# One more seven-product group, the SSM inputs one block earlier, and the samples' attention columns in a lane of their own

## The chip, the cores and the metric

The kernel runs on one core of a Trainium2 chip. The metric is the device time of one execution in microseconds (us); the profiled execution and the timed ones are executions of the same program.

## The reference

One layer of a hybrid decoder trunk, for a prompt of 16 meta tokens and 512 new tokens and for 8 samples of one new token each (536 token columns in all, of which 520 are needed in the output). Everything is float32.

```python
xn = rmsnorm(x, norm_gain)
q, k, v, z_a, u, z_s, g_a, g_s = split(xn @ w_in)        # 2048 -> 8704
q, k = rope(rmsnorm(q)), rope(rmsnorm(k))                  # 16 query heads, 4 key heads, 64 wide
o_attn = sink_attention(q, k, v)          # prompt: window 128 and 16 meta keys; samples: their caches
y_ssm  = s5_branch(u)                     # 64 groups of 16, 64 complex states, scan over time, gelu
y_ssm  = y_ssm * sigmoid(y_ssm @ w_glu + b_glu)
br_a = (o_attn * silu(z_a)) @ w_attn_out
br_s = (y_ssm * silu(z_s)) @ w_ssm_out
y = x + (sigmoid(g_a) * br_a + sigmoid(g_s) * br_s) @ w_out
```

The new keys, values, caches and SSM states are outputs as well.

## The kernel before

**How a product is made.** Weights come from memory in units of 1024 x 128 (a "unit": 8 tiles of 128 x 128). ScalarE rounds a unit to `whi` (line 1019 or 1085), VectorE makes the remainder `wlo` (line 1020 or 1086); the activations are split in the same way. TensorE adds three products, high by high, high by low and low by high, so one block of 128 output columns over 2048 inputs is 96 matmuls of 260 or 268 columns (`mm`, line 1179), and over 1024 inputs 48. Units are made two ahead in three buffers (class `Stream`).

**Groups.** A pair of output blocks over 2048 inputs can be made as a group of seven products instead of eight (class `Quads`, function `quad`, Winograd's form of Strassen's scheme): 7 x 24 = 168 matmuls (line 1415) where two plain blocks have 192. VectorE adds weights for it (line 1084) and makes seven `wlo` instead of four. `NQ` is the number of groups in the input projection; the last product, by w_out, is eight groups.

**The order of the program.** It is written as one main line of matmul blocks:

1. five blocks while x arrives, then `NA` = 4 plain blocks;
2. `NQ` = 16 groups (groups 9 to 12 are the query heads, the others gates);
3. sixteen plain blocks in the order of the string in `ORDER1`: `u` an input block of the SSM branch, `h` a block of keys or values, `x` a gate block;
4. the gate blocks that are left (`while nx < 47`), and the last one by hand;
5. "GLU": 8 blocks over the SSM's output, 48 matmuls each, whose results (`Y2`, made by line 1756, a ScalarE cast and line 1699 on VectorE) are the input of 6; the first unit of 6 needs the eighth of them for its last six matmuls;
6. "sD": 16 blocks by w_ssm_out, 48 matmuls each;
7. "A": 16 blocks by w_attn_out, 48 matmuls each, whose input is the attention's output `oT`, split into `A` (lines 1698 and 1699);
8. eight groups by w_out.

**Background.** The SSM blocks, the attention and the samples' attention are Python generators in three lanes (class `Background`). After every few matmuls the main line calls `bg.step(budget)`; each `yield c` costs c of the credit, and `yield None` ends a lane's turn for this step. The budget is a number per 8 matmul steps (6.4 up to the attention, then `BUDGET2` = 6.0 in 4, `BUDGET3` = 3.4 in 5, `BUDGET4` = 4.8 in 6). It counts matmuls of the main line, not time. Ahead of 7, `bg.drain()` runs whatever is left with no matmul of the main line to go beside it. While `bg.fair` holds, lanes take turns; `attention()` sets it to False, and then the first lane goes ahead of the others.

**The background's parts.** `ssm_consts` and `ssm_block` run for eight blocks; block n is put in line when its `u` block is made. `attention()` begins when they are done and the head norms are made: `values`, `keys`, then for each of 4 key heads `queries` and four blocks. A block (kv, b) is `scores` (lines 816 and 817 on TensorE, in two halves that share one bank of PSUM: ScalarE copies a half at line 820, VectorE masks it at line 822), `softmax` (VectorE lines 828 and 829, ScalarE's four exponentials at 832, VectorE 834 and 839, ScalarE's four scalings at 838), `turn` (TensorE's transposes at 847 and 848, VectorE 851, ScalarE 853 and 857) and `weigh` (TensorE 865, VectorE 870). Scores of a block are issued ahead of `turn` and `weigh` of the block before it. `NDELAY` is a number of steps that the first block waits.

**Samples.** `sample_heads` and `sample_weigh` (16 passes over the key cache, 16 over the value cache, VectorE lines 659 and 660) run in lane 2; the lane is added in `attention()`. At the end of `attention()`, after the last block, `at.sample` loads the result and the gates of the samples (tile `zs`, which shares a buffer with `dV` of the blocks), transposes (line 930) and writes the samples' 8 columns of `oT` (line 935).

Engines run their instructions in the order in which the program issues them; that order is fixed when the program is built.

Of the kernel before, what the change touches and what calls it, by code (L numbers as in the profile page):

```python
# [8 lines left out]
F32 = mybir.dt.float32  # L9
# [5 lines left out]
P = 128  # L15
# [321 lines left out]
def ssm_consts(nc, pool, dram, R, D, ub, a_bT, a_bN, a_cT, e32, d_skip, later, free):  # L337

    v = nc.vector
# [13 lines left out]
    bN, c = R["next"]  # L353
# [55 lines left out]
    yield 1.4  # L409
    yield None  # L410

    kp = R["kp"]
    yield None
    with later():
        for a in range(4):
            for i in range(2):
# [270 lines left out]
class Attn:  # L687
# [225 lines left out]
            with self.later():  # L913
                self.weigh(*self.held, *parts)

    def sample(self, oD):

        nc, pool, v = self.nc, self.pool, self.nc.vector
        o = pool.tile([P, 2, 64], F32, name="o_s", tag="sv")
        for n in range(2):  # L920
            nc.gpsimd.dma_start(out=o[:, n], in_=oD)
        zs = pool.tile([P, 8, 2, 4], F32, name="zs", tag="dV", bufs=1)
        for c in range(2):
            nc.gpsimd.dma_start(out=zs[:, :, c], in_=self.gates[:, :, 260 * c + 256:260 * c + 260].rearrange("b p w -> p b w"))
        yield None
        yield None
        yield None
        ps = self.psum.tile([P, 2, 512], F32, name="aux")
        with self.later():
            nc.tensor.transpose(out=ps[:, 0, 0:128], in_=o.rearrange("p a d -> p (a d)"), identity=self.C["idn"])  # L930
        for e in range(2):
            part = slice(64 * e, 64 * e + 64)
            src = ps[part, 0, 0:128].rearrange("p (c j b e) -> p e b c j", c=2, j=4, e=2)[:, e]
            for c in range(2):
                v.scalar_tensor_tensor(out=self.oT[part, :, c, 256:260], in0=src[:, :, c], scalar=4.0, in1=zs[part, :, c],
                                       op0=ALU.mult, op1=ALU.mult)
        yield 0.0
# [7 lines left out]
BUDGET2, BUDGET3, BUDGET4 = 6.0, 3.4, 4.8  # L945
HIGH = 4000
NLOAD = 3
NDELAY = 4
ATTC = (("kg", 1), ("kgs", 1), ("qg", 1), ("qgs", 1), ("mown", P), ("mprev", P), ("bd64", 4), ("sink", 16))
NXR = 10  # L950
NWARM = 9

NA, NQ = 4, 16
QHEADS = range(9, 13)
XORDER = (list(range(16, 25)) + list(range(16)) + list(range(32, 8 + 2 * NQ)) + list(range(25, 32))
          + list(range(8 + 2 * NQ, 48)))
ORDER1 = [(k, 0) for k in "xuhuhuhuhuxuxuxu"]
for _k in "hu":
    for _n, _i in enumerate([i for i, o in enumerate(ORDER1) if o[0] == _k]):
        ORDER1[_i] = (_k, _n)  # L960
# [139 lines left out]
def trunk(tc, A, O):  # L1100
    nc = tc.nc
# [239 lines left out]
    def heads(i, sb=None):  # L1341
# [22 lines left out]
        def sums():  # L1364
            if i > 3:
                ps = aux.tile([P, 2, 512], F32, name="aux")[:, 0]
            else:
                if "ax" not in S:
                    S["ax"] = aux.tile([P, 2, 512], F32, name="aux")
# [16 lines left out]
    def head_norms():  # L1386
# [7 lines left out]
        def finish():  # L1394
            for r1, dst, p, n in rows:
                r2 = ev.tile([p, n], F32, name="z")
                v.tensor_scalar(out=r1, in0=r1, scalar1=1.0 / 64, scalar2=1e-6, op0=ALU.mult, op1=ALU.add)
                rsqrt_dve(nc, ev, r2, r1, [p, n], "z", "")
                nc.sync.dma_start(out=flat2(dst, n), in_=r2)
            normed.append(1)  # L1400

        return finish

# [2 lines left out]
    def samples():  # L1406
        qk = yield from sample_heads(nc, smpl, dram, smc, C["idn"], rawD, rkD, rqD, S["ax"][:, 1, P:],
                                     lambda: tc.issue_after(bg.last))
        smp.extend(qk)
        smp.extend((yield from sample_weigh(nc, smpl, dram, *qk, A["ssk"], A["kc"], A["vc"], lambda: tc.issue_after(bg.last))))  # L1410

    def product(bank, W, x, first, ps=range(8)):
        for p in ps:
# [177 lines left out]
    for n_, (kind, n) in enumerate(ORDER1):  # L1591
# [9 lines left out]
        if sp is None:  # L1601
# [12 lines left out]
            S["ax"] = S.get("ax") or aux.tile([P, 2, 512], F32, name="aux")  # L1614
            S["bu"] = [aux.tile([P, 512], F32, name=n) for n in ("tr", "wg")] + [S["ax"][:, 0]]
            S["kp"] = S["ax"][:, 1, 0:P]
# [4 lines left out]
        uf = sp.tile([P, 2, CH], F32, name="uf", bufs=1)  # L1621
        with tc.high_priority(offset=HIGH):
            v.tensor_tensor(out=uf, in0=ps, in1=R_, op=ALU.mult)
        uD = dram.tile([P, 2 * CH], F32, name="uD", bufs=8)
        nc.gpsimd.dma_start(out=uD, in_=flat(uf))
        uDs[n] = uD
# [2 lines left out]
    def attention():  # L1629
# [2 lines left out]
            yield None  # L1632
        bg.fair, bg.cap = False, 2.0
        bud[0] = BUDGET2
        bg.add(samples(), lane=2)
        nc.sync.dma_start(out=O["pst"], in_=S["pst"])
        nc.sync.dma_start(out=O["sst"], in_=S["sst"])
        spool.__exit__(None, None, None)
# [29 lines left out]
        for kv in range(4):  # L1668
# [7 lines left out]
                for _ in range(NDELAY):  # L1676
                    yield None
            yield from at.blocks(kv, kv == 3)
        while len(smp) < 3:
            yield None  # L1680
        yield from at.sample(smp[2])
        yield from attended()


# [310 lines left out]
```

## Time and profile before

| | us |
|---|---|
| median of 3 runs (1259.73 to 1260.58) | 1259.96 |
| the profiled execution | 1259.92 |
| its span, first to last instruction | 1258.1 |
| TensorE busy in the span | 1245.8 (99%) |
| VectorE | 986.4 (78%) |
| ScalarE | 632.5 (50%) |
| GpSimd | 324.4 (26%) |

PE is TensorE, DVE VectorE, ACT ScalarE, POOL GpSimd, SP the queue that issues most DMAs. A row of the chain gives start, length, engine, output tile, line and number of instructions; a row of waits gives the waiting instruction, what it waited for, and total us, times and longest us; a row of windows gives, after the stretch, its length and then busy us and number of instructions of PE, PE's weight loads, DVE, ACT and POOL, the granted clock, the DMA share and GB/s; a row of the timeline gives start, length, engine, line, operation, output and input tiles and, in brackets, the idle time before it and what ended it.

### The profile page before, as it was taken

How to read it: one execution, taken by the hardware profiler on the slowest of the kernel's cores; microseconds unless marked ns; L12 is line 12 of the kernel's file. 1: busy time of each engine (PE TensorE's matmuls, PEld its weight loads, DVE VectorE, ACT ScalarE, POOL GpSimd, SP SyncE). 2: the span in 40 equal slices, each digit the busy share in tenths (PEclk: the TensorE clock that was granted, in tenths of full speed). 3: DMA queues.
4: the chain of work that ended last, by engine and by line, in shares of the span. 5: the costliest groups of instructions: out<-in, count | busy, mean ns of one | idle time of the engine just before them, and what ended most of it. 6: DMA issues, size and time to landing. Idle time of an engine off the chain costs nothing.

```text
span 1258.1 us, 26470 instructions
## 1 busy us (share of the span) xinstructions
PE 1245.8 (99%) x10333; PEld 1221.6 (97%) x10333; DVE 986.4 (78%) x1516; ACT 632.5 (50%) x1351; POOL 324.4 (26%) x541
## 2 busy tenths in 40 slices
PE   9999999999999999999999999999999999999998
PEld 9999999999999999999999999999999899999998
DVE  8687878888898756778689858899987477887875
ACT  8554444444445587555552233657665433344342
POOL 0003999940000015337345132112111000000000
PEclk9999999999999999999999999999999999999999
DMA  8544443444464475557556479777667466555441
GB/s 294 198 162 149 138 144 110 143 127 162 153 195 154 144 241 175 176 167 180 170 145 173 124 232 278 244 218 230 215 201 240 151 195 190 166 186 168 143 138 51
DMA packets 99872, 222.42 MB, mean 177 GB/s; under 512 B 17324, under 2 KB 36868, under 8 KB 99716
## 3 DMA queue, kind: packets, MB, share of 16 engines
q1 hardware_dynamic: 86500, 191.97, 47.3%
q0 software_dynamic: 13248, 28.77, 8.9%
q8 instruction: 81, 1.33, 0.4%
q14 instruction: 43, 0.35, 0.1%
HBM read 183.17 MB, written 38.43 MB: 176 GB/s over the span
## 4 chain that ended last, share of the span: by engine, by line
PE 89%; issue 4%; DMA 3%; DVE 2%; POOL 1%; ACT 1%; SPq 0%; DVEq 0%; ACTq 0%; POOLq 0%
PE mm L1179 41%; PE pr L1415 37%; PE mm L1271 2%; PE wg L865 1%; PE aux L1415 1%; PE aux L1179 1%; DMA cache<-in_kc 1%; PE aux L1271 1%; DMA KH<-KH 1%; PE wg L537 1%; PE tr L537 1%; PE aux L816 1%; DMA qD<-x 1%; PE tr L478 0%; PE aux L817 0%
## 5 line engine op out<-in xcount | busy, mean ns | idle before, releaser
L1085 ACT CAST whi<-raw 128x1024 fp32r<-128x1024 f32 x168 | 173.2, 1049 | 167.8 <-DVE raw L1084 68.9
L1086 DVE TENSOR_TENSOR wlo<-raw,whi 128x1024 fp32r<-128x1024 f32 x168 | 206.7, 1251 | 56.4 <-ACT whi L1085 56.0
L1019 ACT CAST whi<-raw 128x1024 fp32r<-128x1024 f32 (+3 forms) x124 | 118.4, 964 | 147.1 <-PE mm L1179 70.7
L1415 PE MATMUL pr<-tau,whi 128*128 128x260 f32 x992 | 180.1, 283 | 0.0
L1179 PE MATMUL mm<-xh,whi 128*128 128x260 f32 (+1 forms) x744 | 172.8, 286 | 0.2 <-ACT xr L1244 0.2
L1179 PE MATMUL mm<-xh,wlo 128*128 128x260 f32 (+1 forms) x744 | 172.2, 285 | 0.0
L1179 PE MATMUL mm<-xl,whi 128*128 128x260 f32 (+1 forms) x744 | 171.8, 285 | 0.0
L1020 DVE TENSOR_TENSOR wlo<-raw,whi 128x1024 fp32r<-128x1024 f32 (+3 forms) x124 | 137.6, 1118 | 32.6 <-ACT whi L1019 32.1
L1415 PE MATMUL pr<-cb,whi 128*128 128x260 f32 x848 | 153.0, 283 | 0.0
L1415 PEld LDWEIGHTS pr<-tau,whi 128*128 128x128 f32 x992 | 152.7, 188 | 0.0
L1415 PE MATMUL pr<-tau,wlo 128*128 128x260 f32 x496 | 139.4, 282 | 0.0
L1415 PEld LDWEIGHTS pr<-cb,whi 128*128 128x128 f32 x848 | 130.8, 188 | 0.2 <-ACT z L1449 0.2
L1179 PEld LDWEIGHTS mm<-xh,whi 128*128 128x128 f32 x744 | 123.6, 188 | 1.6 <-issue 1.2
L1179 PEld LDWEIGHTS mm<-xl,whi 128*128 128x128 f32 x744 | 123.8, 188 | 0.4 <-issue 0.4
L1179 PEld LDWEIGHTS mm<-xh,wlo 128*128 128x128 f32 x744 | 123.4, 188 | 0.2 <-issue 0.2
L1084 DVE TENSOR_TENSOR raw<-raw 128x1024 f32<-128x1024 f32 x95 | 118.7, 1250 | 1.4
L1415 PE MATMUL pr<-cb,wlo 128*128 128x260 f32 x424 | 119.1, 283 | 0.2 <-DVE wlo L1086 0.2
L1415 PE MATMUL pr<-xl,whi 128*128 128x260 f32 x376 | 105.1, 282 | 0.0
L1415 PE MATMUL pr<-xh,wlo 128*128 128x260 f32 x376 | 105.0, 283 | 0.0
L1179 PE MATMUL mm<-Y,whi 128*128 128x260 f32 x576 | 104.4, 287 | 0.3 <-ACT t L1755 0.3
L1415 PE MATMUL pr<-xh,whi 128*128 128x260 f32 x376 | 104.3, 284 | 0.0
L1415 PEld LDWEIGHTS pr<-tau,wlo 128*128 128x128 f32 x496 | 93.1, 188 | 0.0
(432 smaller groups left out, 3022.9 us busy)
## 6 DMA issues: line engine op xcount, KB each, us to landing
raw<-in_w SPq DMA_DIRECT2D x202, 512.0 KB, 4.4
gD<-z SPq DMA_DIRECT2D x36, 260.0 KB, 3.1
t<-gD SPq DMA_DIRECT2D x32, 260.0 KB, 3.4
cache<-in_vc POOLq DMA_DIRECT2D x16, 286.0 KB, 3.4
cache<-in_kc POOLq DMA_DIRECT2D x15, 288.0 KB, 4.8
xr<-in_x SPq DMA_DIRECT2D x16, 268.0 KB, 6.0
xg<-in_x SPq DMA_DIRECT2D x8, 536.0 KB
sbw<-rawD SPq DMA_DIRECT2D x16, 260.0 KB, 6.8
```

The lines of the kernel that those rows point to most:

```text
L537: nc.tensor.matmul(o[n], lhsT=D["CL"][:, 2 * e + n, i, 1:5], rhs=H[:, 2 * e + n, i, 0:140], start=False, stop=(i == 1))
L816: nc.tensor.matmul(ps[:, e, 0:272], lhsT=q, rhs=KH[:, k0:k0 + 272], start=True, stop=False)
L865: nc.tensor.matmul(pv[64 * e:64 * e + 64, 0:256], lhsT=V, rhs=pr[:, e::2], start=(i == 0), stop=(i == len(parts) - 1))
L1019: nc.scalar.copy(out=hi, in_=raw)
L1020: self.dve = nc.vector.tensor_tensor(out=lo, in0=raw, in1=hi.bitcast(F32), op=ALU.subtract).ins
L1084: nc.vector.tensor_tensor(out=o, in0=o, in1=i, op=ALU.add)
L1085: nc.scalar.copy(out=hi, in_=t)
L1086: self.dve = nc.vector.tensor_tensor(out=lo, in0=t, in1=hi.bitcast(F32), op=ALU.subtract).ins
L1179: m = nc.tensor.matmul(ps[:, c, 0:W], lhsT=wt[:, k], rhs=xo(kt, c), start=f, stop=l)
L1271: nc.tensor.matmul(ps[:, c, 0:260], lhsT=wt[:, kt % 8], rhs=xk(xo, kt, c, 8), start=f, stop=l)
L1415: m = nc.tensor.matmul(bank, lhsT=wt[:, p], rhs=x(p, e), start=first and f and p == 0, stop=l and p == 7, skip_group_check=not first and l ...
```

## The change

It moves four things. `NQ` goes from 16 to 17, so two gate blocks that stood in step 4 become a group of step 2; `XORDER` and the layout of the weights follow. The string in `ORDER1` puts each `u` one block earlier (first block of step 3 instead of second), and the PSUM tiles that the SSM shares (`S["ax"]`, `S["bu"]`, `S["kp"]`) are made after the first `u` block. `samples()` is put in lane 2 as soon as the head norms are made, makes its heads while lanes take turns, waits there for `bg.fair` to end, and makes the samples' columns of `oT` itself, in its own pool, as soon as the gates of key head 3 are made; `attention()` waits for that at its end. `NDELAY` goes from 4 to 6.

```diff
@@ ssm_consts
+    yield None
+    while "kp" not in R:
+        yield None
     kp = R["kp"]
-    yield None
@@ Attn.sample
-    def sample(self, oD):
-        nc, pool, v = self.nc, self.pool, self.nc.vector
-        o = pool.tile([P, 2, 64], F32, name="o_s", tag="sv")
+    def sample(self, pool, oD):
+        nc, v = self.nc, self.nc.vector
+        o = pool.tile([P, 576], F32, name="ozs", tag="cache")
+        zs = o[:, 128:192].rearrange("p (b c j) -> p b c j", b=8, c=2)
+        o = o[:, 0:128].rearrange("p (n d) -> p n d", n=2)
         for n in range(2):
             nc.gpsimd.dma_start(out=o[:, n], in_=oD)
-        zs = pool.tile([P, 8, 2, 4], F32, name="zs", tag="dV", bufs=1)
...
-NDELAY = 4
+NDELAY = 6
-NA, NQ = 4, 16
+NA, NQ = 4, 17
-ORDER1 = [(k, 0) for k in "xuhuhuhuhuxuxuxu"]
+ORDER1 = [(k, 0) for k in "uxuhuhuhuhuxuxux"]
@@ head_norms, finish
             normed.append(1)
+            bg.add(samples(), lane=2)
@@ samples
         smp.extend(qk)
+        while bg.fair:
+            yield None
         smp.extend((yield from sample_weigh(...)))
+        while not at.gated(3):
+            yield None
+        yield from at.sample(smpl, smp[2])
+        smp.append(True)
@@ trunk, ORDER1's loop: made after the first u block's uf, not ahead of its matmuls
+        if n == 0:
+            S["ax"] = aux.tile([P, 2, 512], F32, name="aux")
+            S["bu"] = [aux.tile([P, 512], F32, name=nm) for nm in ("tr", "wg")] + [S["ax"][:, 0]]
+            S["kp"] = S["ax"][:, 1, 0:P]
@@ attention
-        bg.add(samples(), lane=2)
...
-        while len(smp) < 3:
+        while len(smp) < 5:
             yield None
-        yield from at.sample(smp[2])
         yield from attended()
```

New line numbers are up to seven higher than old ones: 816, 847, 865 and 1179 of before are 818, 849, 867 and 1182 now, and on VectorE 659, 660, 800, 1699, 1756 and 1768 are 661, 662, 802, 1706, 1763 and 1775.

Where things stand in TensorE's order, counted in matmul instructions of the program from its start (a float32 one counts once):

| | before | now |
|---|---|---|
| the last group of step 2 ends | 3619 | 3781 |
| first product of the SSM's constants (`kp`) | 3830 | 3959 |
| last product of the SSM's eighth block | 5799 | 6061 |
| first scores of the attention | 6160 | 6477 |
| the second GLU block begins | 6518 | 6446 |
| the first sD block begins | 6914 | 6815 |
| last matmul of sD | 7871 | 7773 |
| last `weigh` of the attention | 7835 | 7847 |
| all | 8854 | 8830 |

The first place is TensorE's order at the end of sD, where A begins. `mm<-Y` is sD, `mm<-A` is A; `aux<-KH` and `aux<-KL` are scores, `tr` and `wg<-k_idn` transposes, `wg<-po`, `wg<-pm` and `wg<-pp` a block's `weigh`. Before:

```order
L1179 MATMUL mm<-Y_10688,wlo 128x260 x2
L865 MATMUL wg<-po,dV 64x256 x2
L865 MATMUL wg<-pm,Vm 64x256 x2
L865 MATMUL wg<-pp,V 64x256 x2
L1179 MATMUL mm<-Y_10688,whi 128x260 x4
L1179 MATMUL mm<-Y_10688,wlo 128x260 x2
...
L1179 MATMUL mm<-Y2q,whi 128x260 x2
L1179 MATMUL mm<-Y_10688,wlo 128x260 x2
L1179 MATMUL mm<-A_12788,whi 128x260 x6
```

Now:

```order
L867 MATMUL wg<-pp,V 64x256 x2
L849 MATMUL tr<-k_idn,Pn 128x128 x4
L1182 MATMUL mm<-Y_10636,wlo 128x260
L818 MATMUL aux<-KH_9340,QT_11876 128x272
L819 MATMUL aux<-KL_9344,QT_11876 128x272
...
L849 MATMUL tr<-k_idn,Pn 128x128
L933 MATMUL aux<-k_idn,ozs 128x128
...
L867 MATMUL wg<-po,dV 64x256 x2
L867 MATMUL wg<-pm,Vm 64x256 x2
L867 MATMUL wg<-pp,V 64x256 x2
L1182 MATMUL mm<-A_12692,whi 128x260 x6
```

Before, the last block's `weigh` stood 36 matmuls of sD ahead of A. Now the single sD matmul shown is the last, and 74 matmuls of the attention stand between it and A: scores of the blocks (3, 1), (3, 2) and (3, 3), four sets of transposes, five sets of `weigh`, and the samples' transpose.

The second place is VectorE's order from the last block of GLU (`z<-t,z`, the product with the gate) to its `Y2q`, which sD's first unit needs. Before:

```order
L1756 SCALAR_TENSOR_TENSOR z<-t,z 128x520
L800 TENSOR_TENSOR QT_11102<-sbw,QT_11102 64x512
L829 TENSOR_SCALAR m<-m 128x4
L822 COPY_PREDICATED S<-k_attc,aux 128x2x128
L800 TENSOR_TENSOR QT_11105<-sbw,QT_11105 64x512
L1699 TENSOR_TENSOR Y2q<-z,Y_10688 128x520
```

Now:

```order
L1763 SCALAR_TENSOR_TENSOR z<-t,z 128x520
L662 TENSOR_REDUCE o_s<-cache 128x4
L725 SCALAR_TENSOR_TENSOR sbw<-sbw,k_attc 128x520
L841 TENSOR_TENSOR Pm<-S,den 128x64
L802 TENSOR_TENSOR QT_10399<-sbw,QT_10399 64x512
L726 SCALAR_TENSOR_TENSOR sbw<-sbw,k_attc 128x520
L872 TENSOR_TENSOR oT<-wg,zr 128x2x2x32 x2
L824 COPY_PREDICATED S<-k_attc,aux 128x2x128
L802 TENSOR_TENSOR QT_10432<-sbw,QT_10432 64x512
L1706 TENSOR_TENSOR Y2q<-z,Y_10636 128x520
```

Four rows stood between the two; now there are eight (nine instructions), a pass over the value cache and a query's rope among them. From the first such product of GLU to the eighth VectorE has 89 instructions before and 89 now, but not the same ones: line 659 has four more of the value cache and three fewer of the key cache, line 660 three more of the one and two fewer of the other, lines 723, 724 and 726 one more each, 732 two more, 800 two more; 828, 839 and 903 have one fewer each, 851 two fewer, 870 four fewer (line numbers of before). On TensorE 60 matmuls of the background stand among GLU's second to eighth block before, and 33 now.

More of the change, by code (lines that the diff above doesn't have):

```diff
@@ L1367, in sums @@
             else:
-                if "ax" not in S:
-                    S["ax"] = aux.tile([P, 2, 512], F32, name="aux")
                 ps = S["ax"][:, 1, P:]
@@ L1613, in trunk @@
                 nc.gpsimd.memset(t, 0.0)
-            S["ax"] = S.get("ax") or aux.tile([P, 2, 512], F32, name="aux")
-            S["bu"] = [aux.tile([P, 512], F32, name=n) for n in ("tr", "wg")] + [S["ax"][:, 0]]
-            S["kp"] = S["ax"][:, 1, 0:P]
             bg.add(ssm_states(nc, sc, sp, S, A["h0"]), lane=1)
```

## The prediction

> **What bounds the kernel now.** I read the page's busy times first, then the chain for TensorE's pace, TensorE's waits, windows over the stages, and last the timeline of one attention block. The page:
>
> ```profile
> span 1258.1 us, 26470 instructions
> PE 1245.8 (99%) x10333; PEld 1221.6 (97%) x10333; DVE 986.4 (78%) x1516; ACT 632.5 (50%) x1351; POOL 324.4 (26%) x541
> ```
>
> TensorE is never free for long, so the time is the number of matmuls times their pace, plus the places where TensorE waits. Rows of the chain give the pace and the end of the attention:
>
> ```profile
> 57.80 55.62 PE mm L1179 x464
> 139.04 158.99 PE pr L1415 x1323
> 443.92 7.99 PE aux L1179 x67
> 469.73 0.59 PE aux L417 x16
> 889.40 1.01 PE wg L865 x8
> 982.39 1.45 PE wg L865 x12
> 992.05 0.91 POOL zs L924
> ...
> 998.82 0.63 ACT A L1698
> 999.55 92.65 PE mm L1179 x768
> ```
>
> Both 55.62 / 464 and 158.99 / 1323 are 0.120 us a matmul: a plain block of 96 is 11.5 us, a group of 168 is 20.2 us. The last three rows show why A starts at 999.55: the load of the samples' gates `zs` goes out last, at 992.05, then come the split and TensorE. TensorE's waits between 735 and 1000 us, and three stretches (groups; GLU from the first to the eighth product `z`; around A's start):
>
> ```profile
> PE mm L1179 <- ACT A L1698: 2.4, 1, 2.4
> PE aux L816 <- DVE QT L800: 2.0, 1, 2.0
> PE aux L816 <- DVE S L822: 0.7, 2, 0.5
> ...
> ```
>
> ```profile
> 113.40:437.70 324.30, 324.30 (x2702) 321.51 (x2701) 275.18 (x309) 155.06 (x219) 146.62 (x202) 1.00 0.45 146
> 828.50:878.40 49.90, 49.47 (x404) 46.65 (x403) 46.99 (x91) 32.60 (x88) 10.08 (x14) 1.00 0.73 223
> 950.00:1000.00 50.00, 47.57 (x389) 43.92 (x387) 26.13 (x52) 23.25 (x69) 4.88 (x8) 1.00 0.59 191
> ```
>
> VectorE is busy 46.99 of 49.9 us in GLU (94%), where TensorE still does not wait. So there are two places with little to spare: VectorE in GLU, and whatever is left of the attention when sD ends, since nothing of the main line covers it. Both meet the change.
>
> **The change part by part.** The sum goes against the profiled execution, 1259.9 us; the median of the runs is 1259.96, so no correction.
>
> *The seventeenth group.* Two plain blocks of 192 matmuls become 168: 24 x 0.120 = -2.9 us. Its three extra casts, three extra `wlo` and four weight sums lie beside 20.2 us of matmuls, on a VectorE that is busy 275 of 324 us in that stage and a ScalarE busy half of it: nothing. If that cover failed, a group would be late by the wait for one `wlo`, about 1 us.
>
> *What the group takes away.* Those two blocks stood where the attention runs. The budget is counted in matmuls, so the background gets 2 x 2 x 6.0 = 24 us of credit less behind the groups. The `u` blocks one earlier should give half of it back, but the order shows they don't: the SSM's last product stands 2280 matmuls behind the end of the groups now and 2180 before, the first scores 1370 ahead of A's start instead of 1711, and 74 matmuls of the attention are left when sD is over. That is the drain. TensorE there has to wait for ScalarE and VectorE, whose work on one block is, in the timeline (ScalarE, then VectorE, then TensorE):
>
> ```profile
> 971.97 0.40 ACT L820 COPY S<-aux 128x288 f32<-128x288 f32 x1 [1.97 <-PE aux L817]
> 974.43 0.42 ACT L832 ACTIVATE S<-S,m 128x145 f32<-128x145 f32 x1 [2.06 <-DVE m L829]
> ...
> 975.95 0.19 ACT L832 ACTIVATION_READ_ACCUMULATOR S<-S,m 128x1 f32 x1
> 976.05 0.56 ACT L857 COPY pp<-tr 128x512 f32<-128x512 f32 x1
> 976.51 1.04 ACT L1019 CAST whi<-raw 128x1024 fp32r<-128x1024 f32 x1
> 977.46 0.99 ACT L838 ACTIVATE Pn<-S,den 128x128 f32<-128x128 f32 x3
> 978.35 1.11 ACT L853 ACTIVATE pm<-wg,k_attc 64x128 f32<-64x128 f32 x4
> ```
>
> ```profile
> 972.40 0.45 DVE L822 COPY_PREDICATED S<-k_attc,aux 128x256 f32<-128x256 int32 x1 [1.61 <-ACT S L820]
> 972.96 0.76 DVE L828 TENSOR_REDUCE m<-S 128x4 f32<-128x580 f32 x1
> 973.75 0.49 DVE L870 TENSOR_TENSOR oT<-wg,zr 128x128 f32<-128x128 f32 x2
> 974.15 0.16 DVE L829 TENSOR_SCALAR m<-m 128x4 f32<-128x4 f32 x1
> 974.33 0.69 DVE L851 TENSOR_TENSOR po<-tr,k_attc 128x512 f32<-128x512 f32 x1
> 976.49 0.17 DVE L834 RECIPROCAL den<-den 128x4 f32<-128x4 f32 x1
> 976.95 0.22 DVE L839 TENSOR_TENSOR Pm<-S,den 128x64 f32<-128x64 f32 x1 [0.29 <-PE wg L848]
> ```
>
> ```profile
> 957.66 0.28 PE L816 MATMUL aux<-KH,QT 128*128 128x272 f32 x1
> ...
> 958.15 0.28 PE L1179 MATMUL mm<-Y2q,whi 128*128 128x260 f32 x1
> 973.63 0.66 PE L847 MATMUL tr<-k_idn,Pn 128*128 128x128 f32 x4
> ```
>
> ScalarE's queue from the end of sD on: six copies of scores (2.4), four times four exponentials (974.43 to 976.14, 1.7 each: 6.8), four sets of scalings (1.3 each: 5.1), five `pm` (5.6), four `pp` (2.3), one weight cast (1.0) and the first split (0.6): 23.8 us without a gap, the lower end. One block alone, nothing overlapped, is two halves of scores at 1.65 (TensorE 0.5, 0.40, 0.45 and hand-overs), 0.9 to the maximum and its scaling, 1.7, 0.4 on VectorE, 1.3, transposes 0.7, 1.8 for `pm` and `po`, 1.45 of `weigh`, 0.5: 12 us; three of these and 2 us for block (2, 3) are 38, the upper end. Going through the rows in their order, each starting when its engine and its input are there, I come to 29 us from sD's last matmul to A's first; it lies nearer the lower end because scores of the next block stand ahead of a block's `turn`. Of these 29 us TensorE's own rows are 12 (six halves at 0.49; `weigh` four times 1.45 and once 1.01; transposes and `Pm` about 2.5), which it did before as well, under cover. So the drain costs 17 us net, between 12 and 26.
>
> *Waits that go.* A's 2.4 us (the old end of the attention) are replaced by the drain: -2.4. The 2.0 us for the first `QT` goes, since two more steps of delay put 48 matmuls, 5.8 us, ahead of those scores: -2.0, or 0. The 0.7 us at scores and what is smaller I leave as they are.
>
> *GLU.* Its eight blocks now carry other background. TensorE from the first to the eighth product `z`: 336 matmuls are 40.4 us, and 33 background ones (24 of scores at 0.123, a `weigh`, transposes) 4.5: 45 us, where 60 stood before and it took 49.2. VectorE's 89 instructions there add up to 2.1 us more than before (four cache multiplies of 0.75 for three of 0.76, reductions, rope at 0.75, `QT` at 0.69, less `po`, `oT`, a maximum): 49 to 51 us. It falls behind by 4 to 6 us. Before, it ran behind by about 4 throughout (`z` after its tanh; the last row, of a table by line, is the cache multiply's mean):
>
> ```profile
> 823.41 0.69 ACT L1755 ACTIVATE t<-mm,k_bglu 128x520 f32<-128x520 f32 x1
> 828.51 0.69 DVE L1756 SCALAR_TENSOR_TENSOR z<-t,z 128x520 f32<-128x520 f32 x1
> ...
> 873.39 0.71 ACT L1755 ACTIVATE t<-mm,k_bglu 128x520 f32<-128x520 f32 x1
> 877.71 0.70 DVE L1756 SCALAR_TENSOR_TENSOR z<-t,z 128x520 f32<-128x520 f32 x1
> 880.43 0.70 DVE L1699 TENSOR_TENSOR Y2q<-z,Y 128x520 fp32r<-128x520 f32 x1
> ...
> L659 DVE TENSOR_TENSOR cache<-cache,ssc 128x572 f32<-128x572 f32 x16 | 11.6, 749 | 0.0
> ```
>
> The last `Y2q` came 2.0 us behind its `z`; the rows between them now add up to 4.9. So it is ready 0.7 + 0.7 + 5.3 us plus the lag behind GLU's end, and sD's first unit needs it after 42 matmuls and 9 of the background, 6 us. With a lag of 4 to 10 TensorE waits 4.5 to 10.5 us, once, at sD's beginning; I take 7, with 3 to 10 as ends.
>
> *`u` first.* The constants' first product came 25.8 us behind the end of the groups (469.73 - 443.92), behind 210 matmuls or 25.2 us; now 178 or 21.4 stand ahead of it. If the loads and casts for it take as long as before TensorE waits up to 4.4 us; nothing if they follow the order. I take 1, since much of that chain begins with the groups' end in both.
>
> *Samples' lane.* Their columns no longer stand behind the last block. On GpSimd's queue the result's load goes out after the two copies of the windows, as before, six blocks ahead of its use: hidden. If it were late, TensorE's transposes behind the samples' one would wait with it in the drain. No instruction is added; the wait in lane 2 is one of the builder, not of an engine.
>
> Sum: 1259.9 - 2.9 - 2.4 - 2.0 + 17 + 7 + 1 = 1277.6. I say 1277 us.
>
> A rule of the Trainium skill bears on both waits. In the trace the granted clock is 1.00 in every window, also in the one with the 2.4 us wait. The skill (TensorE: Matmul & The Clock Gate, "What's actually happening") says that an idle window of about 3.4 us halves TensorE's clock until a busy window has passed. By it a single wait of 7 us, and perhaps the drain, would each be followed by some 3.4 us at half rate, an estimated 1.7 us each, so 1279 to 1281; no run here has a wait that long.
>
> **The rivals.** *The drain is as cheap as blocks were before* (the other side). The sixteen blocks before made TensorE wait 0.7 us for masked scores, and if the handing over in the drain cost no more, its 12 us of rows would take 13: 1277.6 - 16 = 1261.6. It decides below a net drain of 1.9 us, where the time comes within 0.2% of before. For it: the rows are the same ones. Against it: from 889.40 to 982.39 eight blocks took 11.6 us each then, filled with sD; ScalarE alone needs 23.8. 5 in 100.
>
> *VectorE catches up in GLU.* It was idle 6% of that stretch; if the lag at GLU's first block is nil and rows overlap better, sD's first unit finds `Y2q` ready: 1270.6, with the drain's ends 1266 to 1279. 20 in 100.
>
> *The drain is serial*: in-order queues line the blocks up, 38 us, net 26: 1286.6. For it: both halves of scores share one bank, and ScalarE's copy of the next half often stands behind `pm` or the exponentials. 12 in 100.
>
> *The clock falls.* If TensorE ran at half its pace for as long as the wait at sD's beginning lasted, 7 us hold 29 matmuls instead of 58: +3.5, and as much behind the drain: up to 1284.6. Against it: 1.00 everywhere so far. 10 in 100.
>
> **How the numbers follow.** The forecast with both waits (1271 to 1284) has 53 in 100. Cases that end above 1262.5 are slower by more than 0.2% (2.5 us, about what this kernel's measurement tells from no change): all but the first rival's 5 in 100, of which 4 lie in the band and 1 below it (a drain that cheap with a lag absorbed too), and one more below it for what I have not seen: slower 0.94, same 0.04, faster 0.02. The range 1266 to 1288 leaves out the first rival and the tails of the second and third.
>
> **What would show it.** Groups: 168 matmuls more at line 1423 (and 192 fewer at 1182), same pace. The chain at the end of sD through ScalarE and VectorE, with TensorE's waits on scores, `Pn` and `pm` and 25 to 33 us from sD's last matmul to A's first. A wait of TensorE on VectorE's `Y2q` (line 1706) at sD's beginning. No wait on `zs`. Wrong would be: A within 20 us of sD's end, or no wait at sD's beginning and a low lag of `z`.

## The result, and the profile after

The changed kernel takes 1274.32 us (median of four runs, 1272.49 to 1276.49) where the kernel before took 1260.06 beside it: ratio 1.0113, 95% interval 1.0095 to 1.0132. The profiled execution took 1275.33 us, a span of 1273.6, 15.5 more than before. The page's first lines:

```profile
span 1273.6 us, 26432 instructions
PE 1248.9 (98%) x10309; PEld 1222.0 (96%) x10309; DVE 995.2 (78%) x1526; ACT 635.8 (50%) x1358; POOL 320.3 (25%) x541
```

TensorE has 24 matmuls fewer than before, as the group should have it (1056 rows of `pr<-tau,whi` for 992), and yet it is busy 3.1 us longer. Its idle time, span less busy, went from 12.3 to 24.7 us. So the 15.5 us are 12.4 of new waits, less 2.9 for 24 matmuls at 0.120, which leaves 6.0 for rows that ran slower. Stage by stage, first before, then after: from the groups' end to GLU's first matmul; GLU and sD; from sD's last matmul to A's first (columns as before: length, busy us and number for PE, PE's weight loads, DVE, ACT, POOL, then granted clock, DMA share, GB/s):

```profile
443.90:811.70 367.80, 365.05 (x3075) 359.58 (x3073) 281.39 (x543) 192.95 (x569) 146.02 (x281) 1.00 0.66 193
811.70:997.10 185.40, 184.74 (x1497) 170.46 (x1495) 149.14 (x287) 114.15 (x326) 27.81 (x45) 1.00 0.67 211
997.10:999.50 2.40, 0.01 (x1) 0.00 (x0) 1.20 (x5) 0.68 (x2) 0.00 (x0) 1.00 0.12 6
```

```profile
464.10:805.10 341.00, 335.83 (x2846) 332.10 (x2844) 260.15 (x505) 173.36 (x521) 150.33 (x287) 1.00 0.67 189
805.10:986.80 181.70, 178.38 (x1437) 167.53 (x1438) 150.06 (x281) 107.49 (x293) 21.51 (x40) 0.99 0.73 232
986.80:1014.90 28.10, 18.06 (x103) 10.49 (x101) 14.44 (x43) 20.66 (x78) 0.38 (x2) 0.88 0.20 66
```

The groups end 20.2 us later (one group more); the first stage shown is 26.8 us shorter, the second 3.7, and the time from A's first matmul to the end is the same (258.6 and 258.7). The third is the drain: 28.1 us for 2.4, with 18.06 us of TensorE in it and a granted clock of 0.88. Of the 12.4 us of idle time 7.6 lie in the drain, 2.4 ahead of GLU and 2.7 in GLU and sD. TensorE's waits, over the whole span:

```profile
PE mm L1182 <- ACT Y L1705: 4.6, 1, 4.6
PE wg L850 <- DVE Pm L841: 2.3, 2, 1.2
PE aux L818 <- DVE S L824: 2.0, 2, 1.1
PE aux L818 <- DVE QT L802: 1.8, 1, 1.8
...
PE tr L480 <- DMA kD<-k: 0.6, 1, 0.6
```

The largest is new and was not forecast: GLU's first block waits 4.6 us for `Y1`, the SSM's output. Its loads go out when the last gate block has done with `xl`, and the rest of that block covers them: 9.9 us before (801.8 to 811.7, with rows of the attention in it), 6.9 now (793.6 to 800.45, with none of them). They also land later. The same four of the eight loads, with the casts that ScalarE makes of them, before and then after (least, median and greatest ns of one, then the first and the last start in us):

```profile
L1731 SPq DMA_DIRECT2D Y<-yD x4: 382/470/937, 802.3 to 804.2; - x4
L1698 ACT CAST Y<-Y x4: 625/628/632, 807.4 to 811.1; 128x520 fp32r<-128x520 f32 x4
```

```profile
L1738 SPq DMA_DIRECT2D Y<-yD x4: 320/490/693, 794.0 to 796.7; - x4
L1705 ACT CAST Y<-Y x4: 617/622/625, 804.4 to 808.3; 128x520 fp32r<-128x520 f32 x4
```

The first of them was cast 5.1 us behind its issue before, without a wait for it; now it is cast 10.4 us behind, as soon as it is there, and TensorE starts when that cast ends. The profile's row of DMA issues has the landing of the four after (KB each, median us):

```profile
Y<-yD SPq DMA_DIRECT2D x4, 260.0 KB, 10.7
```

So 3 us of cover are gone and some 5 us of landing came on top; before, that cast had ended 3.7 us ahead of GLU's first matmul. Together they make the wait. What the clock did in and after that wait (windows of after):

```profile
800.45:805.10 4.65, 0.06 (x1) 0.00 (x0) 2.95 (x5) 1.29 (x3) 0.00 (x0) 1.00 1.25 292
805.10:806.80 1.70, 1.69 (x6) 1.41 (x7) 1.70 (x3) 1.43 (x2) 0.00 (x0) 0.50 0.97 334
806.80:808.50 1.70, 1.70 (x10) 1.70 (x10) 1.70 (x4) 1.28 (x3) 0.00 (x0) 0.51 1.06 403
808.50:810.20 1.70, 1.70 (x16) 1.70 (x16) 1.70 (x4) 1.70 (x4) 0.00 (x0) 1.00 1.02 396
```

In the wait the DMA share is 1.25; over the loads of before (801.8 to 809.5) it was 0.98, so much traffic alone does not tell the two apart. Behind the wait 3.4 us run at a clock of 0.50, in which 16 matmuls start where 28 fit: another 1.5 us. The drain's beginning and end in the timeline:

```profile
986.41 0.36 PE L1182 MATMUL mm<-Y,wlo 128*128 128x260 f32 x1
...
1010.60 1.12 PE L867 MATMUL wg<-po,dV 128*64 128x256 f32 x4 [0.87 <-DVE po L853]
1011.48 1.10 PE L867 MATMUL wg<-pm,Vm 128*64 128x256 f32 x4
1012.33 1.09 PE L867 MATMUL wg<-pp,V 128*64 128x256 f32 x4
1014.89 1.20 PE L1182 MATMUL mm<-A,whi 128*128 128x260 f32 x6 [1.48 <-issue]
```

28.1 us lie between sD's last matmul and A's first, and the last `weigh` takes 2.8 us (1010.60 to 1013.42) where twelve such matmuls took 1.45 before. The samples' columns are out of the way: the transpose on `ozs` waits for nothing.

### The profile page after: what moved, and what is told of

Its sections match the earlier page's. It is cut to its first block, busy times and chain, and to the rows that moved or that the text cites. A ratio compares the mean times of both kernels' runs of the same rounds, so it can differ in the third digit from the quotient of the medians.

```text
span 1273.6 us, 26432 instructions
## 1 busy us (share of the span) xinstructions
PE 1248.9 (98%) x10309; PEld 1222.0 (96%) x10309; DVE 995.2 (78%) x1526; ACT 635.8 (50%) x1358; POOL 320.3 (25%) x541
## 4 chain that ended last, share of the span: by engine, by line
PE 83%; DMA 7%; DVE 3%; issue 3%; ACT 2%; SPq 1%; POOL 1%; DVEq 0%; POOLq 0%; ACTq 0%
PE pr L1423 38%; PE mm L1182 36%; PE wg L867 2%; PE aux L1423 1%; DMA raw<-in_w 1%; DMA Y<-yD 1%; DMA xr<-in_x 1%; DMA sbw<-rawD 1%; DMA uD<-uf 1%; PE aux L818 1%; PE tr L849 1%; PE wg L539 1%; PE tr L539 1%; DMA U<-uD 1%; DMA out_k<-sbw 0%
## 5 line engine op out<-in xcount | busy, mean ns | idle before, releaser
L1089 DVE TENSOR_TENSOR wlo<-raw,whi 128x1024 fp32r<-128x1024 f32 x175 | 215.1, 1251 | 59.7 <-ACT whi L1088 59.1
L1423 PE MATMUL pr<-tau,whi 128*128 128x260 f32 x1056 | 191.7, 283 | 0.0
L1182 PE MATMUL mm<-xh,whi 128*128 128x260 f32 (+1 forms) x696 | 162.3, 286 | 1.0 <-ACT xr L1247 1.0
L1423 PEld LDWEIGHTS pr<-tau,whi 128*128 128x128 f32 x1056 | 162.6, 188 | 0.0
L1182 PE MATMUL mm<-xl,whi 128*128 128x260 f32 (+1 forms) x696 | 161.9, 285 | 0.0
L1182 PE MATMUL mm<-xh,wlo 128*128 128x260 f32 (+1 forms) x696 | 161.1, 285 | 0.0
L1423 PE MATMUL pr<-tau,wlo 128*128 128x260 f32 x528 | 148.5, 283 | 0.0
L1182 PEld LDWEIGHTS mm<-xh,whi 128*128 128x128 f32 x696 | 115.9, 188 | 2.0 <-ACT xr L1247 1.3
L1182 PEld LDWEIGHTS mm<-xl,whi 128*128 128x128 f32 x696 | 116.3, 188 | 0.4 <-issue 0.4
L1182 PEld LDWEIGHTS mm<-xh,wlo 128*128 128x128 f32 x696 | 115.4, 188 | 0.7 <-issue 0.6
```

Source lines behind the costliest of these rows:

```text
L1089: self.dve = nc.vector.tensor_tensor(out=lo, in0=t, in1=hi.bitcast(F32), op=ALU.subtract).ins
L1182: m = nc.tensor.matmul(ps[:, c, 0:W], lhsT=wt[:, k], rhs=xo(kt, c), start=f, stop=l)
L1423: m = nc.tensor.matmul(bank, lhsT=wt[:, p], rhs=x(p, e), start=first and f and p == 0, stop=l and p == 7, skip_group_check=not first and l ...
```

## The experiments

The theory of the prediction ("credit") was that the seventeenth group takes two blocks' worth of credit from the background, and that this leaves the drain. Its rival ("turns") was formed from the order of the changed kernel: the samples' heads, entered as soon as the head norms are made, take turns from the SSM, whose last product then stands 2280 matmuls behind the groups instead of 2180. All twelve runs in one table (each ratio is to runs of the kernel before beside it, whose medians were 1260.06 to 1261.68); "room" is the number of matmuls from the attention's first scores to sD's last matmul in TensorE's order, "left" those of the attention behind it, both counted from the built program (some expectations give "left" up to 9 too low).

| kernel | room | left | sD to A, us | median, us | ratio to before |
|---|---|---|---|---|---|
| before | 1711 | 0 | 2.4 | 1260.06 | |
| after: group, u ahead, lane, delay 6 | 1296 | 74 | 28.1 | 1274.32 | 1.0113 (1.0095 to 1.0132) |
| e7: u ahead alone | 1802 | 0 | 0 | 1256.49 | 0.9962 (0.9949 to 0.9976) |
| e3: group alone | 1432 | 23 | 19.1 | 1284.83 | 1.0189 (1.0172 to 1.0206) |
| e12: lane alone | 1418 | 38 | 15.8 | 1270.5 | 1.0077 (1.0062 to 1.0091) |
| e6: group, u ahead | 1603 | 7 | 9.5 | 1264.21 | 1.0024 (1.0014 to 1.0033) |
| e2: u ahead, lane, delay 6 | 1566 | 7 | 4.8 | 1260.41 | 0.9996 (0.9986 to 1.0005) |
| e1: after, samples entered later | 1601 | 6 | 3.8 | 1262.33 | 1.0011 (1.0002 to 1.0021) |
| e5: e1 with more credit | 1607 | 0 | 0.3 | 1263.95 | 1.0018 (1.0009 to 1.0027) |
| e4: after with more credit | 1324 | 46 | 17.8 | 1274.53 | 1.0101 (1.0086 to 1.0116) |
| e11: after with delay 4 | 1320 | 50 | 21.6 | 1274.23 | 1.0103 (1.0089 to 1.0117) |
| e8: after, caches behind the gates | 1441 | 38 | 34.8 | 1283.78 | 1.0178 (1.0164 to 1.0192) |
| e9: e7 with delay 14 | 1665 | 0 | 3.0 | 1263.9 | 1.0021 (1.0012 to 1.003) |
| e10: after, rows added in the drain | 1296 | 170 | 36.4 | 1282.46 | 1.0165 (1.0151 to 1.0179) |

**e1, the samples entered later.**

```diff
@@ head_norms, finish
-            bg.add(samples(), lane=2)
@@ attention
         bud[0] = BUDGET2
+        bg.add(samples(), lane=2)
```

> The changed kernel (17 groups, u ahead, samples in a lane of their own), but the samples' lane is entered where it was entered before, when the attention begins, and so not while the SSM still takes fair turns. Theory 'credit' (the prediction's: the seventeenth group takes two blocks' credit from the background): the group is still there, so the drain should stay, 20 us or more from sD's last matmul to A's first, and 1268 to 1276 us. Theory 'turns' (the samples' heads, entered early, take turns from the SSM, the SSM ends later and everything behind it starts later): in this kernel's order the SSM's last product stands 2080 matmuls behind the groups instead of 2280 and only some 6 matmuls of attention are left behind sD; the drain shrinks to 4 to 8 us and the time is 1259 to 1265 us, on the lower side if the wait of 4.6 us on Y1 at GLU's beginning goes as well.

1262.33 us. This one line, moved, takes 12 us off the changed kernel (13 against the kernel before beside each). In the order the SSM ends 185 matmuls earlier and the scores begin 237 earlier; the 28.1 us of drain are 3.8, and the wait on `Y1` is 0.5. "Turns" holds, with a drain just under its 4 to 8 us. The group is still there, so "credit" fails as the cause of the whole drain. What remains against before are other waits:

```profile
PE aux L818 <- DVE QT L802: 3.4, 1, 3.4
PE aux L818 <- DVE S L824: 2.3, 2, 1.5
PE mm L1182 <- issue: 1.9, 1, 1.9
```

**e2, sixteen groups.**

```diff
-NA, NQ = 4, 17
+NA, NQ = 4, 16
```

> The changed kernel with 16 groups instead of 17; u ahead and the samples' lane are kept. Theory 'credit': without the seventeenth group the background has its two blocks back, the drain goes: 1260 to 1263 us. Theory 'turns': the samples still take turns from the SSM (last product 2270 matmuls behind the groups), but the groups end 162 matmuls earlier, so 7 matmuls are left behind sD: also a short drain, 4 to 8 us, 1262 to 1267 us. The two differ by what is left of the drain and by whether e1 comes out alike.

1260.41 us, no difference from before that the interval shows. The time lies in the range of "credit", under that of "turns"; the drain, 4.8 us, lies in that of "turns". No wait exceeds 1.5 us. So this run does not decide between the two, and it shows that the group has a part in the drain. The lane entered early does little harm where there is room: the group and the lane each push the attention back, and together it is too much.

**e3, the group alone**, in the kernel before.

```diff
-NA, NQ = 4, 16
+NA, NQ = 4, 17
```

> The kernel before with only the seventeenth group. Theory 'credit': nearly the whole cost is here: a drain of 20 us or more and 1270 to 1277 us. Theory 'turns': the group alone moves the SSM's end by 231 matmuls, but the attention catches up all but its last 17 matmuls (two of its blocks are weighed behind sD): a drain of 6 to 12 us in place of the 2.4 us, 1262 to 1268 us.

1284.83 us, the slowest of all, above both expectations, and the drain is near the 20 us of "credit", not the 6 to 12 of "turns". Only 23 matmuls are left behind sD, yet the drain is 19.1 us, and TensorE waits 7.3 us on the first `QT` far ahead of it. The waits of this kernel:

```profile
PE aux L816 <- DVE QT L800: 7.3, 1, 7.3
PE wg L848 <- DVE Pm L839: 3.9, 1, 3.9
PE aux L930 <- DMA o_s<-oD: 3.4, 1, 3.4
```

and its drain in the windows, where 37 matmuls take 19.2 us at a clock of 0.70:

```profile
1002.50:1021.70 19.20, 6.84 (x37) 3.75 (x35) 7.76 (x21) 7.82 (x25) 4.64 (x7) 0.70 0.56 184
```

In the chain 7.8 us lie between the last `weigh` shown and A, and the samples' columns fill most of them, since they are made behind the last block. Without them the last product on VectorE (ending at 1016.15) and the split would still be there, so an estimate of their cost from these rows is 4.7 us:

```profile
1012.72 1.14 PE wg L865 x4
...
1014.14 0.91 POOL zs L924
...
1017.50 2.77 DMA zs<-gD
...
1020.96 0.63 ACT A L1698
...
1021.68 0.56 PE mm L1179
```

By itself the group is the dearest part of the change, not by its own work but by what it pushes back: the SSM's last product stands 231 matmuls later in the order than before. Of the 24.6 us by which this span is longer than before's, 17.4 are idle time of TensorE; its rows, 24 fewer, take 7.2 us longer, so about 10 us are slower rows, at a mean granted clock of 0.988 for 1.000.

**e4, more credit beside sD.**

```diff
-BUDGET2, BUDGET3, BUDGET4 = 6.0, 3.4, 4.8
+BUDGET2, BUDGET3, BUDGET4 = 6.0, 3.4, 6.4
```

> The changed kernel with the last budget raised from 4.8 to 6.4 per eight steps, so a third more credit for the attention beside sD. Theory 'credit': the attention catches up, the drain goes, 1257 to 1263 us. Theory 'turns': the attention starts as late as before (first scores at the same place) and its blocks then follow one another at ScalarE's and VectorE's pace, not the credit's; 40 instead of 65 matmuls are left in the order: the drain is 17 to 23 us instead of 28, 1266 to 1271 us.

1274.53 us, the time of after: "credit" is wrong, and "turns" expected too much here. The drain is shorter as "turns" said (17.8 us), but in the profile sD ends 6.5 us later. That execution, 1271.51 us, was 3 us below the other three of this kernel, so its drain may be flattered. Credit beside sD moves rows from the drain to sD; it does not make the chain of the attention shorter. No run gave more credit ahead of the attention, beside the SSM, where the group takes it.

**e5, e1 with more credit**: budgets 4.4 and 6.0 in place of 3.4 and 4.8.

> The kernel of e1 (17 groups, u ahead, the samples' lane entered when the attention begins) with the two budgets beside GLU and sD raised from 3.4 and 4.8 to 4.4 and 6.0. In its order the last weigh stands 14 matmuls ahead of sD's last one, where in e1 6 matmuls were behind it. Theory 'start' (what the attention costs is set by when it begins, and credit only shifts its last blocks): the 3.8 us between sD and A falls to 2 to 3 us, all else stays: 1260 to 1262 us. Theory 'credit': the attention is what holds the end up, and with more of it the time goes below the kernel before by the whole gain of the group: 1256 to 1259 us.

1263.95 us, no better than e1 (their intervals overlap), and above both expectations. The drain is gone (0.3 us), but GLU and sD take 190.9 us for 186.2, with a wait of 1.8 on `pm` (0.4 in e1); the waits on `QT` (3.8) and `S` (1.8) stand as in e1 (3.4 and 2.3). A drain of 4 us was not the thing to remove.

**e6, group and u ahead**, the samples as before: e3 with u ahead (and the SSM's tiles made behind the first `u`, as in the change).

```diff
-NA, NQ = 4, 16
+NA, NQ = 4, 17
-ORDER1 = [(k, 0) for k in "xuhuhuhuhuxuxuxu"]
+ORDER1 = [(k, 0) for k in "uxuhuhuhuhuxuxux"]
```

> The kernel before with the seventeenth group and u ahead, but with the samples treated as before (their columns of the output behind the last block). Theory 'start': the SSM's last product is where it is in e1 (2080 matmuls behind the groups), the first scores as well, so the time is e1's, 1261 to 1265 us, and u ahead takes back some 20 us of what the group alone cost (1284.8). Theory 'columns' (the end of the attention is held up by the samples' columns, whose result came 3.4 us late in e3's drain, and the lane is what removes that): the drain stays near e3's 19 us less the late start, 1268 to 1275 us.

1264.21 us: moving `u` one block ahead takes back 20.6 of the 24 us. "Start" holds. A part of "columns" holds too: A waits 7.8 us, and the chain shows the load of `zs` in it, as in e3. The lane removes that (e1: 1.9).

```profile
PE mm L1181 <- ACT A L1699: 7.8, 1, 7.8
```

**e7, u ahead alone** (the edit of e6 with `NQ` at 16).

> The kernel before with u ahead alone: 16 groups, samples as before. In the order the SSM ends 90 matmuls earlier than before, and the last weigh stands 172 matmuls ahead of sD's end instead of 36. Theory 'start': nothing of the attention is left at sD's end, A's wait of 2.4 us and the 2.0 us for the first QT shrink or go: 1255 to 1259 us. If those waits are set by something else (a transfer, VectorE's queue): 1259 to 1261 us, no change.

1256.49 us, ratio 0.9962: faster than both kernels, as expected, and the best of the study. A follows sD without a wait. The wait on `QT` did not go, it grew to 3.6 us.

**e8, the samples' caches behind the gate blocks.**

```diff
@@ samples
-        while bg.fair:
+        while bg.fair or nx < 48:
             yield None
```

> The changed kernel, but the samples' walk over their caches begins only when the last gate block is done, so that its four loads of 288 KB do not fall into the 780 to 812 us stretch in which Y's loads took 10.7 us to land and TensorE waited 4.6 us on Y1. Theory 'traffic' (Y's loads are slow because the transfers of the attention and of the samples share the engines with them): landing falls below 5 us and the wait on Y1 to under 1.5 us. Rival (the loads are slow because of the keys' copies and weights alone, or issued late): landing stays above 8 us and the wait at 3 us or more. The order also leaves only 32 instead of 65 matmuls behind sD's end, so the drain should be 14 to 20 us in both, and the time 1260 to 1267 by the first and 1264 to 1270 us by the second.

1283.78 us, outside every time given. For the question it asked "traffic" holds in the main: without the samples' loads in that stretch Y's loads land in 5.6 us (under 5 was expected) and the wait on `Y1` is 0.6. The scores begin 109 matmuls earlier as well, so more than the samples' loads was moved. But the walk over the caches, begun so late, ends late, and its result is waited for in the drain:

```profile
PE aux L933 <- DMA ozs<-oD: 9.5, 1, 9.5
```

So the walk over the caches cannot be put off that far; in e1, where it begins with the attention, nothing waits for it.

**e9, e7 with a later first score.**

```diff
-NDELAY = 4
+NDELAY = 14
```

> The kernel of e7 (before with u ahead alone, 1256.5 us) with the delay of the first scores raised from 4 to 14 steps. In e7 TensorE waited 3.6 us on the first QT, and its attention ended 172 matmuls ahead of sD's end, so there is room: in this order the first scores stand 137 matmuls (16 us) later and the last weigh still 66 ahead of sD's end. Theory 'start' (the first scores stand too early for their QT, and nothing else waits): the wait goes, 1252 to 1254 us. Rival (the attention pushed into GLU meets VectorE, which is the reason that a late attention is dear): what is won at QT is lost beside GLU and sD, 1255 to 1259 us.

1263.9 us, 7.4 above e7; the rival holds and "start" as I put it fails. The wait on `QT` is gone, and a longer one stands in its place: 8.4 us at a later score. The row names `m`, which ends at 797.46, but what frees the bank of the scores is the masked copy (`S`, line 824), which ends at 797.42. VectorE's queue ahead of it (timeline of VectorE, then TensorE's row):

```profile
778.50 0.76 DVE L661 TENSOR_TENSOR cache<-cache,qv 128x576 f32<-128x576 f32 x1 [3.96 <-DMA cache<-in_kc]
...
785.21 0.76 DVE L661 TENSOR_TENSOR cache<-cache,qv 128x576 f32<-128x576 f32 x1 [2.70 <-DMA cache<-in_kc]
...
792.12 0.76 DVE L661 TENSOR_TENSOR cache<-cache,qv 128x576 f32<-128x576 f32 x1 [1.77 <-DMA cache<-in_kc]
...
796.98 0.44 DVE L824 COPY_PREDICATED S<-k_attc,aux 128x256 f32<-128x256 int32 x1
```

```profile
797.47 0.59 PE L818 MATMUL aux<-KH,QT 128*128 128x272 f32 x1 [8.36 <-DVE m L831]
```

VectorE sits idle on loads of the samples' caches, in order, with the masking of scores queued behind them. So here a late attention is dear because its first scores meet the caches on VectorE's queue (GLU begins only at 818.7), besides the wait of 3.0 us on A.

**e10, TensorE kept busy in the drain**: 24 transposes of the identity behind the transposes of each of the last four blocks.

```diff
@@ turn, behind its transposes
+        if kv == 3:
+            for r in range(24):
+                nc.tensor.transpose(out=pv[:, 384:512], in_=C["idn"], identity=C["idn"])
```

> The changed kernel with 24 transposes of the identity, into columns that nothing reads, behind the transposes of each of the last four attention blocks: 96 more rows on TensorE, 6 us of them, all in the drain, where TensorE is busy 18 of 28 us and its granted clock 0.88. Theory 'clock' (the waits of the drain lower the clock, and the slow rows lengthen its chain): with the gaps filled the granted clock of the drain goes to 0.95 or more, the real rows there take their usual time (a weigh of four 0.60 to 0.65 us instead of 1.1), and the drain is 2 to 4 us shorter: 1270 to 1273 us. Rival (the chain through ScalarE and VectorE sets the drain, TensorE's pace in it does not matter): the drain stays at 27 to 30 us whatever the clock, 1273 to 1277 us. If the added rows get in the way: up to 6 us longer.

1282.46 us, 8 more than after. The clock of the drain rose to 0.95 and from 998 us on every set of four `weigh` matmuls took 0.60 to 0.65 us, so the clock does follow the gaps; but each set of 24 takes 2.8 us and stands ahead of the rows that the chain needs:

```profile
985.60:1022.00 36.40, 27.47 (x199) 20.05 (x197) 14.24 (x43) 21.20 (x78) 0.38 (x2) 0.95 0.16 52
```

What the slow clock costs in the drain can't be read from this run, since the added rows lengthened the chain by more.

**e11, the delay back at four** (`NDELAY = 4` in the changed kernel).

> The changed kernel with the delay of the first scores back at 4 steps. The prediction had the two more steps take away the 2.0 us for QT; they did not (1.8 us stayed). Theory 'start' (the first scores stand behind the SSM's end and the keys, not behind the delay): the first scores stand at the same place in the order (matmul 6473), the wait on QT stays between 1.5 and 3 us, and 42 instead of 65 matmuls are left behind sD: a drain of 17 to 24 us, but as in e4 little of it in the time: 1271 to 1275 us. If the delay does matter: a wait on QT of 4 us or more and 1275 to 1279 us.

1274.23 us, as after: the wait on `QT` is 1.7 us with either delay. The drain is 6.5 us shorter, for a later end of sD (992.1 for 986.8), and without gain: the clock was at half for most of it and for the first 3.4 us of A:

```profile
992.10:1013.80 21.70, 14.44 (x70) 8.54 (x68) 10.26 (x30) 14.73 (x50) 0.19 (x1) 0.69 0.19 61
1013.80:1017.20 3.40, 3.40 (x16) 3.40 (x17) 3.40 (x6) 3.40 (x7) 0.00 (x0) 0.50 0.52 159
```

**e12, the lane alone**, in the changed kernel with 16 groups, the old string and the delay of 4.

> The kernel before with the samples' lane alone (entered early, their columns made in it): 16 groups, u where it was, a delay of 4. Theory 'turns' (samples entered beside the SSM push its end back; a late attention is what costs): the SSM's last product stands 205 matmuls later than before, nearly as with the group alone (231), and 34 matmuls are left behind sD: a drain of 13 to 20 us and 1268 to 1276 us. Rival (what made the group alone so dear, 1284.8, is mostly the samples' result that came late behind the last block, and with the columns in their own lane a late attention costs little): at most 1264 us.

1270.5 us: "turns" holds. The lane entered early costs 9 us with no seventeenth group about, with a drain of 15.8 us and 2.3 us on `Y1`. The SSM's last product stands 2390 matmuls behind the groups, 210 later than before.

## Why the prediction was right, and where it was wrong

The time and its sign came out (1277 predicted, 1274.3 measured), on terms of which some were wrong.

- **Group, -2.9.** Right: same pace, 168 matmuls more and 192 fewer, VectorE and ScalarE hidden.
- **Drain, 29 us to A.** The size was right: 28.1 us, through ScalarE, VectorE and TensorE's waits in it, on `Pm` (2.3), `wlo` (1.7), `m` (1.4) and `S` (1.1) above all; none on `Pn` or `pm`, which the prediction named. With the 12 us of rows that the prediction counted in it, 16.1 net for 17. But only 10.0 of these are waits: TensorE is busy 18.06 us there, 6 more than counted, with a granted clock of 0.54 over 989.1 to 992.5 and 0.70 to 0.77 over 1008.5 to 1014.9. The sum had no term for slow rows, so part of the agreement is luck.
- **Its cause.** Wrong as the whole of it: "the background gets 24 us of credit less". The group does push the attention back (e3), but with the group in place and the samples entered later the drain is 3.8 us (e1), and more credit beside sD (e4) buys nothing. What sets the drain is how early the attention begins, which hangs on the SSM's end. "The `u` blocks one earlier should give half of it back, but the order shows they don't" failed as well: they give back nearly all (e3 to e6, 20.6 us), and the early entry of the samples, which the prediction costed at nothing, takes it again (e1 to after, 12 us). I read the sum of two moves as one. The step that failed is the one on the samples' lane: it looked at its columns, its queue and its use, not at whose turns it takes.
- **A's wait on `zs`, -2.4.** Right: it is gone.
- **`QT`, -2.0.** Wrong: 1.8 us stayed. The delay moves nothing there (e11), because the keys and queries follow the SSM's end, and the first scores are at the same place with a delay of 4 or 6.
- **GLU, +7 as a wait on `Y2q` at sD's beginning.** Wrong in its place. From the first to the eighth `z` VectorE took 50.2 us, as worked out (49 to 51), and the last `Y2q` came 5.3 us after its `z`. But `z` fell behind its tanh by 2.7 us more (1.2 at the first, 3.9 at the eighth), not by 4 to 6, since TensorE took longer as well: 47.5 us between these two tanh, for 45. And the program has 42 matmuls of sD's second unit and 23 of the attention ahead of the first unit's last six, so TensorE had work. The two units' results leave the bank together, which shows it (timeline):

```profile
869.33 0.68 DVE L1763 SCALAR_TENSOR_TENSOR z<-t,z 128x520 f32<-128x520 f32 x1
874.62 0.70 DVE L1706 TENSOR_TENSOR Y2q<-z,Y 128x520 fp32r<-128x520 f32 x1
878.30 1.29 DVE L1775 SCALAR_TENSOR_TENSOR z<-t,mm 128x520 f32<-128x520 f32 x2
```

  The order before has rows of the second unit there too (21); the prediction counted only the first unit's 42 and 9 of the background, and so had too little cover. In its stead TensorE waited at GLU's beginning on `Y1`: 4.6 us and 1.5 of slow clock, which no step had. About the same size, by chance.
- **`u` first, +1.** 0.6 on `kD`, as a wait; what it is worth downstream was missed (above).
- **The clock.** A rival at 10 in 100, not in the sum: it came true in part, and most of the 6.0 us of slower rows go to it (the mean granted clock of the span is 0.996 for 1.000, an estimated 5 us). By the rule quoted in the prediction (the Trainium skill, TensorE: Matmul & The Clock Gate, "What's actually happening") an idle window of about 3.4 us halves the clock until a busy window has passed, for one such wait an estimated loss of 1.7 us; the trace agrees for the wait on `Y1`, with 3.4 us at 0.50 and 1.5 us lost. In the drain, whose waits are all under 1.8 us, the clock fell too; the last section has more such cases.

The sum 17.7 held since a missing 7 was replaced by the wait on `Y1`, the slow clock and what stayed of `QT`.

## What to carry to other kernels

When a change moves several things, work out for each alone where it puts the start of the longest dependent chain: here u ahead (-0.4%), the group (+1.9%) and the lane (+0.8%) each act, as far as the order and the waits show, mostly by moving the attention's beginning, and they do not add up. A generator entered into a fair scheduler costs those it shares turns with, even when it adds no instruction. And a larger budget for the background beside sD bought nothing in e4 and e5: where the chain starts late, move its start, not its share.

## What the runs showed of the hardware

- After a single long wait of TensorE the granted clock is 0.50. After waits of 3.4 us (e1), 3.6 (e7), 4.6 (after), 7.8 (e6) and 8.4 (e9) this lasts about 3.4 us, and then the clock is 1.00; after 3.8 (e5) it lasts 5.1 us and after 7.3 (e3) 7.0. Shorter waits go both ways: after 2.7 (e6) and 2.3 (e12) the clock is 0.50 and 0.52 for 3.4 us, beginning more than 1 us behind the wait (784.0 and 807.0), and after 2.0 and 2.4 (before) and 3.0 (e9) it stays at 1.00. So in these runs the length of the wait does not decide it alone. e7's rows, the wait first:

```profile
759.80:763.40 3.60, 0.01 (x1) 0.00 (x0) 3.54 (x7) 2.28 (x3) 0.00 (x0) 0.98 0.75 242
763.40:765.10 1.70, 1.67 (x7) 1.67 (x8) 1.67 (x3) 0.24 (x1) 0.00 (x0) 0.50 0.04 15
...
766.80:768.50 1.70, 1.70 (x17) 1.70 (x16) 1.67 (x3) 1.63 (x4) 0.00 (x0) 1.00 1.09 298
```

- The clock also falls without a long wait. In e11's drain no wait is over 2.1 us; it fell after 3.4 us with TensorE 1.36 us busy (40%), and a stretch at 0.50 with 2.68 of 3.4 us busy (79%) did not bring it back. A low busy share does not always bring it down either: with 0.97 of 3.4 us busy (before, 996.2 to 999.6) and 0.40 (e9, 1000.2 to 1003.6) it stayed at 1.00. What share decides is not shown. Windows of e11:

```profile
996.60:1000.00 3.40, 1.36 (x11) 0.79 (x9) 1.86 (x7) 2.36 (x11) 0.00 (x0) 1.00 0.48 189
...
1002.30:1005.70 3.40, 2.68 (x12) 1.37 (x12) 1.86 (x4) 1.88 (x8) 0.00 (x0) 0.50 0.00 0
```

- The same four loads of 260 KB from `yD` landed in 10.7 us in the changed kernel, at a DMA share of 1.13 around them (795 to 810), and in 5.6 in e8, where the samples' loads are not there and the share is 1.00.
